# Sums of raw weight blocks on GpSimd instead of VectorE in a hybrid decoder layer

## The chip, the cores and the metric

The kernel runs on one core of a Trainium2 chip. A core has four compute engines with a queue of their own each: TensorE (PE in the profile; its weight loads are PEld), VectorE (DVE), ScalarE (ACT) and GpSimd (POOL). SyncE (SP) issues the loads from memory. Every engine works through its queue in order, and instructions of different engines wait for each other by semaphores. The metric is the device time of one execution in microseconds, as the median of several runs.

## The reference, cut to what matters

One layer of a hybrid decoder on 256 tokens of width 2048: a recurrent branch and an attention branch side by side, merged by gates, then a SwiGLU block and a gated per-layer input. Nearly all of the work is products of activations (256 rows) with large float32 weight matrices:

```
h = rmsnorm(x, g_mix[i])
proj = h @ w_in[i]
x_r, g_r, q, k, v, gate_r, gate_a = jnp.split(proj, IN_SPLIT_POINTS, axis=-1)
...
y_r = y_r @ w_rnn_out[i]
...
x = x + mix @ w_o[i]
h = rmsnorm(x, g_ffn[i])
gu = h @ w_ffn_gu[i]
g, u = jnp.split(gu, 2, axis=-1)
x = x + (jax.nn.silu(g) * u) @ w_ffn_down[i]
ple_gate = jax.nn.sigmoid(rmsnorm(x, g_ple[i]) @ w_ple_gate[i])
x = x + ple_gate * (p[i] @ w_ple_proj[i])
```

## The kernel before, in words

**Weights in two parts.** Every weight block is loaded as float32 by SyncE in chunks of up to 128 x 1024 (tile `w`, four buffers). ScalarE makes a rounded high part of it (`whi`, line 233) and VectorE the low part, weight minus high part (`wlo`, line 234); there are four buffers of each. TensorE then forms each product out of three matmuls, high by high, high by low, low by high (lines 496 to 498 in `prod`). High and low parts of a chunk are made in program order three chunks ahead of TensorE's use (`need`: the 3 is `ahead_split`), and loads run four chunks further ahead (`ahead_dma`). So a chunk's high part can start once TensorE has finished the chunk four places earlier and given its buffers back.

**Groups and slots.** In the token-major stages a group makes 256 tokens x 1024 columns of an output. It is a list of slots, each of which uses one chunk. A slot with a number is a row block of the weights of 128 x 1024: four products (two column halves, two token halves), twelve matmuls. In a group with seven products, four row blocks and their eight quarters are multiplied in the way of Strassen and Winograd: instead of eight products of blocks there are seven, of sums of blocks. These are the slots with letters; each has two products, six matmuls:

```
SEVEN = [0, 1, 2, 3, "11", 8, "21", 9, "22", 10, "T1", 11, "T2", 12, "T3", 13, "T4", 14, 15]
```

`SEVEN_FIRST` has "11", "21" and "22" next to each other, `LONG` has the lettered slots after four numbered ones and more numbered ones behind. The groups with seven products are the two of the recurrent output (`ro`, with `LONG`), two of v, two of the output projection (`wo`), eleven of gate and up (`gu`) and the first of the per-layer gate (`pg`): 18 groups.

**The sums of raw blocks.** The four quarter blocks 11, 21, 22 and 12 (the last is loaded in slot T1) lie in four tiles named X, of a ring of seven. `summed` (line 206) gives the block whose parts a slot needs. For 11, 21 and 22 that is the block as loaded. For T1 to T4 it first adds two tiles in place: T1 is R = 11 + 12, T2 is R = R + 22, T3 is 12 = 12 + 22, T4 is R = R + 21, with R the tile of 11. Line 217 is this addition, over 128 x 1024 float32. Since R is written in place, the sum for T1 must wait until the parts of 11 have been made, the one for T2 until those of T1 have, and the one for T4 until those of T2 have; T3 writes the tile of 12 and must only come behind T1. `split_to` then makes the parts of the result. The order on each engine is laid by the tile framework's scheduler, which may put an instruction ahead of others of its queue when it is ready early.

Other work on these engines in the same stretch: VectorE adds the products' results out of PSUM (line 301, the helper `tt`) and scales them (line 304, `stt`); ScalarE applies Silu, Sigmoid, squares and copies (line 307, `actv`). In the first recurrent output group VectorE also finishes the last recurrent gates (`rnn_gates`, lines 636 to 646).

Of the kernel before, what the change touches and what calls it, by code (L numbers as in the profile page):

```python
# [11 lines left out]
ALU = mybir.AluOpType  # L12
# [162 lines left out]
class Stream:  # L175
# [30 lines left out]
    def summed(self, mode):  # L206


        r = self.raw
        if mode[0] != "T":  # L210
            if mode == "11":
                r["R"] = r["11"]
            return r[mode]
        if mode == "T1":
            r["12"] = r["T1"]
        o, a = {"T1": ("R", "12"), "T2": ("R", "22"), "T3": ("12", "22"), "T4": ("R", "21")}[mode]
        self.nc.vector.tensor_tensor(r[o], r[o], r[a], ALU.add)  # L217
        return r[o]

    def split_to(self, n):  # L220
# [884 lines left out]
```

## Time and profile before

| | |
|---|---|
| median of 3 runs | 1898.63 us (1896.6 to 1898.97) |
| span of the profiled execution | 1897.5 us |
| TensorE busy | 1885.3 us |
| VectorE busy | 1356.5 us |
| ScalarE busy | 1114.1 us |
| GpSimd busy | 2.2 us, 9 instructions |
| sums of line 217 | 72, 88.0 us on VectorE |

The profile is of one execution. A timeline row gives start and duration in us, engine, line of the kernel, operation, what is written and read, how many instructions the row holds, and in brackets the idle time before it and what ended that. A row of groups ends with busy time, mean ns of one, and idle time before. A row of waits reads: engine and what waited, for whom, total us, times, longest. A row of windows gives a stretch, its length, the busy us of PE, PEld, DVE, ACT and POOL with their instructions, the granted clock of TensorE as a share of full speed, the DMA engines' busy share and GB/s.

### The profile page before, as it was taken

Reading aid. Unit: us, or ns where it says so; the run is one execution under the profiler, and the core shown is the slowest. Engines: PE = TensorE matmul, PEld = TensorE weight load, DVE = VectorE, ACT = ScalarE, POOL = GpSimd, SP = SyncE. Lnnn points to the kernel's source line nnn. Section 1 sums busy time; section 2 is a strip of 40 time slices with the busy share of each in tenths; the row PEclk is TensorE's granted clock in tenths of the full one; section 3 lists DMA queues with packets and bytes.
Section 4 is the critical chain, followed back from the end, with each engine's and each line's share of the span. In section 5 each row is a group of like instructions: output and inputs, shape, how many; then the busy total and the mean of one; then the engine's idle time right before and its main releaser. Section 6 shows DMA issues by size and latency. Waiting matters only on the chain.

```text
span 1897.5 us, 24029 instructions
## 1 busy us (share of the span) xinstructions
PE 1885.3 (99%) x9045; PEld 1585.9 (84%) x9045; DVE 1356.5 (71%) x1618; ACT 1114.1 (59%) x1447; POOL 2.2 (0%) x9
## 2 busy tenths in 40 slices
PE   8999999999999999999999999999999999999998
PEld 7988888888888888888888888888888888888887
DVE  7867686877787576665568888865786577865784
ACT  6878686874455576676345755543554355544663
POOL 0000000000000000000000000000000000000000
PEclk9999999999999999999999999999999999999999
DMA  6555555656554554545575555565556555555654
GB/s 238 183 200 182 197 178 194 209 186 217 212 185 168 189 165 156 166 158 175 195 269 183 184 199 191 199 219 178 188 189 223 188 188 189 177 178 191 220 161 149
DMA packets 101781, 361.37 MB, mean 190 GB/s; under 512 B 11424, under 2 KB 11808, under 8 KB 101664
## 3 DMA queue, kind: packets, MB, share of 16 engines
q1 hardware_dynamic: 101520, 359.82, 56.0%
q8 instruction: 71, 1.16, 0.2%
q14 instruction: 46, 0.38, 0.1%
q10 hardware_dynamic: 144, 0.01, 0.0%
HBM read 357.69 MB, written 2.10 MB: 190 GB/s over the span
## 4 chain that ended last, share of the span: by engine, by line
PE 97%; DVE 1%; DMA 1%; ACT 1%; issue 0%; SPq 0%; DVEq 0%; ACTq 0%
PE ps L497 26%; PE ps L498 26%; PE ps L496 26%; PE ps L426 8%; PE ps L430 4%; PE ps L409 1%; PE ps L410 1%; PE ps L408 1%; DMA w<-in_w_dram 1%; PE ps L995 1%; PE ps L786 0%; PE ps L935 0%; DVE wlo L234 0%; DVE T L301 0%; ACT L307 0%
## 5 line engine op out<-in xcount | busy, mean ns | idle before, releaser
L234 DVE TENSOR_TENSOR wlo<-w,whi 128x1024 fp32r<-128x1024 f32 (+3 forms) x606 | 731.7, 1215 | 383.8 <-ACT whi L233 382.0
L233 ACT ACTIVATE whi<-w 128x1024 fp32r<-128x1024 f32 (+3 forms) x606 | 635.9, 1053 | 585.5 <-PE ps L498 515.1
L497 PE MATMUL ps<-wlo,B 128*128 128x512 f32 x1130 | 441.5, 391 | 0.7 <-DVE wlo L234 0.7
L498 PE MATMUL ps<-whi,B 128*128 128x512 f32 x1130 | 441.0, 390 | 0.0
L496 PE MATMUL ps<-whi,B 128*128 128x512 f32 x1130 | 390.5, 393 | 0.1
L497 PE MATMUL ps<-wlo,A 128*128 128x512 f32 x946 | 369.6, 391 | 0.0
L498 PE MATMUL ps<-whi,A 128*128 128x512 f32 x946 | 368.6, 390 | 0.0
L496 PE MATMUL ps<-whi,A 128*128 128x512 f32 x946 | 353.0, 392 | 0.0
L496 PEld LDWEIGHTS ps<-whi,B 128*128 128x128 f32 x1130 | 212.3, 188 | 43.9 <-ACT whi L233 0.6
L498 PEld LDWEIGHTS ps<-whi,B 128*128 128x128 f32 x1130 | 212.3, 188 | 43.9
L497 PEld LDWEIGHTS ps<-wlo,B 128*128 128x128 f32 x1130 | 212.5, 188 | 43.6 <-DVE wlo L234 1.1
L498 PEld LDWEIGHTS ps<-whi,A 128*128 128x128 f32 x946 | 177.8, 188 | 36.6
L497 PEld LDWEIGHTS ps<-wlo,A 128*128 128x128 f32 x946 | 177.9, 188 | 36.1 <-DVE wlo L234 0.4
L496 PEld LDWEIGHTS ps<-whi,A 128*128 128x128 f32 x946 | 177.8, 188 | 35.9
L233 ACT ACTIVATE whi<-X 128x1024 fp32r<-128x1024 f32 x126 | 133.7, 1061 | 70.0 <-PE ps L498 57.8
L426 PE MATMUL ps<-A,whi 128*128 128x512 f32 x704 | 172.1, 394 | 1.6 <-ACT whi L233 1.6
L234 DVE TENSOR_TENSOR wlo<-X,whi 128x1024 fp32r<-128x1024 f32 x126 | 154.2, 1224 | 24.5 <-ACT whi L233 21.7
L426 PEld LDWEIGHTS ps<-A,whi 128*128 128x128 f32 x704 | 129.9, 190 | 26.8 <-ACT whi L233 2.1
L301 DVE TENSOR_TENSOR T<-ps,T 128x512 f32<-128x512 f32 (+1 forms) x160 | 91.1, 611 | 27.6 <-ACT T L307 16.7
L430 PEld LDWEIGHTS ps<-A,wlo 128*128 128x128 f32 x704 | 90.6, 191 | 7.3 <-DVE wlo L234 3.7
L430 PE MATMUL ps<-A,wlo 128*128 128x256 f32 x704 | 92.3, 284 | 3.1 <-DVE wlo L234 2.7
L217 DVE TENSOR_TENSOR X<-X,X 128x1024 f32<-128x1024 f32 x72 | 88.0, 1222 | 1.4
(158 smaller groups left out, 1421.4 us busy)
## 6 DMA issues: line engine op xcount, KB each, us to landing
w<-in_w_dram SPq DMA_DIRECT2D x584, 512.0 KB, 3.8
X<-in_w_dram SPq DMA_DIRECT2D x72, 512.0 KB, 4.6
w<-in_w_dram SPq DMA_DIRECT2D x16, 448.0 KB, 3.3
C<-in_x_dram SPq DMA_DIRECT2D x8, 256.0 KB, 4.2
out_dram<-T SPq DMA_DIRECT2D x8, 256.0 KB, 3.3
C<-in_xT_dram SPq DMA_DIRECT2D x7, 256.0 KB, 7.9
w<-in_w_dram SPq DMA_DIRECT2D x4, 320.0 KB, 3.6
w<-in_w_dram SPq DMA_DIRECT2D x2, 256.0 KB, 3.2
```

Source lines behind the costliest of these rows:

```text
L217: self.nc.vector.tensor_tensor(r[o], r[o], r[a], ALU.add)
L233: self.hi_ins = self.nc.scalar.activation(hi[:, :c], t[:, :c], AF.Copy)
L234: self.lo_ins = self.nc.vector.tensor_tensor(lo[:, :c], t[:, :c], hi[:, :c].bitcast(F32), ALU.subtract)
L301: nc.vector.tensor_tensor(o, a, b, op)
L408: nc.tensor.matmul(o, wt[0], xh, start=start, stop=False)
L409: nc.tensor.matmul(o, wt[0], xl, start=False, stop=False)
L410: nc.tensor.matmul(o, wt[1], xh, start=False, stop=stop)
L426: nc.tensor.matmul(pss[e], wt[0], rhs(xs, k), start=(k == 0), stop=(k == n - 1))
L430: nc.tensor.matmul(pss[e][:, :256], wt[1], rhs(xs, k)[:, :256], start=False, stop=False)
L496: nc.tensor.matmul(ps, x[0], wh, start=start, stop=False)
L497: nc.tensor.matmul(ps, x[0], wl, start=False, stop=False)
L498: nc.tensor.matmul(ps, x[1], wh, start=False, stop=stop)
```

## The change

The addition of line 217 is issued on GpSimd's queue instead of VectorE's. Operands, shapes, order of the calls and everything else stay.

```
         o, a = {"T1": ("R", "12"), "T2": ("R", "22"), "T3": ("12", "22"), "T4": ("R", "21")}[mode]
-        self.nc.vector.tensor_tensor(r[o], r[o], r[a], ALU.add)
+        self.nc.gpsimd.tensor_tensor(r[o], r[o], r[a], ALU.add)
         return r[o]
```

## The prediction

> **What bounds the kernel now.** I read the busy table of the page first, then the chain of waits, then who waited for whom.
>
> ```profile
> span 1897.5 us, 24029 instructions
> ...
> PE 1885.3 (99%) x9045; PEld 1585.9 (84%) x9045; DVE 1356.5 (71%) x1618; ACT 1114.1 (59%) x1447; POOL 2.2 (0%) x9
> ...
> PE 97%; DVE 1%; DMA 1%; ACT 1%; issue 0%; SPq 0%; DVEq 0%; ACTq 0%
> ...
> L217 DVE TENSOR_TENSOR X<-X,X 128x1024 f32<-128x1024 f32 x72 | 88.0, 1222 | 1.4
> ```
>
> TensorE is busy for 99% of the span and makes 97% of the chain. So the 88.0 us that leave VectorE (72 sums, L217) are not in the time today, except where TensorE waits for VectorE. The list of waits shows how little that is:
>
> ```profile
> ACT whi L233 <- PE ps L498: 572.9, 424, 2.8
> ACT whi L233 <- DVE X L217: 3.7, 3, 1.9
> PE ps L497 <- DVE wlo L234: 0.7, 1, 0.7
> ```
>
> TensorE waited once for a low part in a token-major stage, 0.7 us. ScalarE waited 424 times for TensorE to give a buffer back: the splits run as far ahead as four buffers allow. ScalarE waited for a sum three times, 3.7 us. The change can therefore win next to nothing; the question is whether the slower path eats the lead of the splits.
>
> **The lead in a usual group.** The timeline of VectorE and ScalarE in the fourth group of the gate and up stage, around T2 and T4:
>
> ```profile
> 1225.03 1.23 DVE L234 TENSOR_TENSOR wlo<-X,whi 128x1024 fp32r<-128x1024 f32 x1
> 1226.29 1.23 DVE L217 TENSOR_TENSOR X<-X,X 128x1024 f32<-128x1024 f32 x1
> 1227.75 1.23 DVE L234 TENSOR_TENSOR wlo<-w,whi 128x1024 fp32r<-128x1024 f32 x1 [0.24 <-ACT whi L233]
> 1229.15 1.23 DVE L234 TENSOR_TENSOR wlo<-X,whi 128x1024 fp32r<-128x1024 f32 x1 [0.18 <-ACT whi L233]
> 1230.42 1.22 DVE L217 TENSOR_TENSOR X<-X,X 128x1024 f32<-128x1024 f32 x1
> 1232.10 1.22 DVE L234 TENSOR_TENSOR wlo<-w,whi 128x1024 fp32r<-128x1024 f32 x1 [0.46 <-ACT whi L233]
> ...
> 1226.65 1.06 ACT L233 ACTIVATE whi<-w 128x1024 fp32r<-128x1024 f32 x1 [1.66 <-PE ps L498]
> 1228.06 1.06 ACT L233 ACTIVATE whi<-X 128x1024 fp32r<-128x1024 f32 x1 [0.34 <-PE ps L498]
> ```
>
> Low part of T1, sum for T2 (R += 22) at 1226.29, low part of slot 11, low part of T2, sum for T4, low part of slot 12. ScalarE's high parts wait for TensorE, that is, for the buffer of four slots earlier. Between that and the use of the new parts lie three slots. TensorE starts a product's three matmuls every 0.68 us:
>
> ```profile
> 1880.05 0.39 PE L496 MATMUL ps<-whi,B 128*128 128x512 f32 x1
> ...
> 1880.73 0.39 PE L496 MATMUL ps<-whi,B 128*128 128x512 f32 x1
> ```
>
> A numbered slot has four products, 2.72 us, a lettered one two, 1.36 us. A numbered slot between lettered ones is thus split 1.36 + 2.72 + 1.36 = 5.44 us ahead and needs 1228.98 - 1226.65 = 2.33 us: a margin of 3.1 us. A lettered one has 6.8 us ahead, a margin of 4.5 us.
>
> **Part one: 72 sums leave VectorE.** In the usual group they lie under TensorE's work (margin above), so removing them is worth nothing there; VectorE was not late. In the first group of the recurrent output it is late:
>
> ```profile
> 406.07 1.23 DVE L234 TENSOR_TENSOR wlo<-X,whi 128x1024 fp32r<-128x1024 f32 x1 [2.48 <-ACT whi L233]
> 407.21 0.42 DVE L636 TENSOR_SCALAR T<-T 128x512 f32<-128x512 f32 x1
> 407.55 1.22 DVE L217 TENSOR_TENSOR X<-X,X 128x1024 f32<-128x1024 f32 x1
> 408.68 1.22 DVE L234 TENSOR_TENSOR wlo<-w,whi 128x1024 fp32r<-128x1024 f32 x1
> 409.82 1.22 DVE L217 TENSOR_TENSOR X<-X,X 128x1024 f32<-128x1024 f32 x1
> 410.95 0.69 DVE L304 SCALAR_TENSOR_TENSOR T<-T,T 128x512 f32<-128x512 f32 x1
> 411.55 1.22 DVE L234 TENSOR_TENSOR wlo<-X,whi 128x1024 fp32r<-128x1024 f32 x1
> ...
> 410.47 0.39 PE L497 MATMUL ps<-wlo,B 128*128 128x512 f32 x1
> ...
> 415.85 0.51 PE L497 MATMUL ps<-wlo,B 128*128 128x512 f32 x1 [0.66 <-DVE wlo L234]
> ```
>
> Here the low part of slot 4 (408.68 to 409.90) is read at 410.47: a margin of 0.57 us. A little later TensorE stands still for 0.66 us. Two sums, T1 and T3, stand in this queue, 1.14 us from start to start each. If they went away at no cost, TensorE would win that 0.66 us.
>
> **Part two: 72 sums on GpSimd.** No sum of this form has run there. Its nearest rows:
>
> ```profile
> L352 POOL MEMSET w1l<- 128x512 f32 x1 | 0.6, 607 | 0.0
> L352 POOL MEMSET w1h<- 128x512 f32 x1 | 0.5, 524 | 0.3 <-POOLq L1093 0.3
> L363 POOL TENSOR_SCALAR_AFFINE_SELECT negt<-T 128x256 f32<-128x256 f32 x1 | 0.4, 401 | 0.0
> L357 POOL TENSOR_SCALAR_AFFINE_SELECT T<-ones 128x128 f32<-128x128 f32 x1 | 0.3, 288 | 0.0
> ```
>
> Below: VectorE's 1.22 us. The two selects give (401 - 288) / 128 = 0.88 ns per column, so 1024 columns of one input take 1.08 us, of two inputs read one after the other some 2.0 us. Above: the slower memset, 607 / 512 = 1.19 ns per column, once for each of two reads and a write: 3.6 us. I take 2.44 us, twice VectorE's row and the middle of 1.2 and 3.6. The Trainium skill (GPSIMD Engine Reference, Elementwise — side-by-side cycle accounting) gives 4497 ns for an add of 2048 columns; half of it is an estimate of 2.25 us, by which the sum below would be 0.4 us less.
>
> **Part three: do the two engines hinder each other?** GpSimd's sum and VectorE's low part each read two SBUF tiles. The trace has no such pair. Bounds: no hindrance, or each stops the other for its whole length. The only hint is in the first microseconds:
>
> ```profile
> 0.80 0.52 POOL L352 MEMSET w1h<- 128x512 f32 x1 [0.29 <-POOLq L1093]
> 1.26 0.61 POOL L352 MEMSET w1l<- 128x512 f32 x1
> ...
> 1.10 0.30 DVE L348 CAST ones_r<-ones 128x128 fp32r<-128x128 f32 x1
> 1.32 0.27 DVE L360 MEMSET T<- 128x256 f32 x1
> ```
>
> The second memset, with more of VectorE's work beside it, took 0.09 us longer than the first. I take the exclusive end, since it is these reads that would meet. The Trainium skill (SBUF — State Buffer, Who interferes with whom) speaks against this change in the same sense: a VectorE instruction with two SBUF inputs and a GpSimd instruction that reads SBUF share one read interface, whoever starts first keeps it for the whole instruction, and the other is blocked. No row of this trace shows it; by that rule the time is the one below, without it that of the first rival.
>
> Usual group, exclusive: the sum for T2 holds VectorE from 1226.29 to 1228.73, so slot 11's low part is 1.0 us late and T2's high part, due at 1228.06, 0.7 us. T2's low part ends about 1231.1, the sum for T4 runs to 1233.5, slot 12's low part is 1.4 us late. All below 3.1 us: no stall, price nothing. In letters with D for the sum, the last delay is 2D - 3.5; it passes 3.1 at D = 3.3.
>
> First group of the recurrent output, exclusive: the low part of 11 ends at 407.30; T1's sum runs to 409.74, T3's to 412.18, and slot 4's low part starts then instead of at 408.68, 3.5 us late against a margin of 0.57: TensorE stalls 2.9 us. The next low part keeps the 0.69 us instruction in front of it but has lost a sum (1.14 us), so what follows is 3.5 - 1.14 = 2.4 us late, and the 0.66 us stall of before is taken up in it. Net: 2.4 us.
>
> Such a stall has a second price. Early in the run TensorE stood still for 1.87 us, and the granted clock of the stretch after it was halved:
>
> ```profile
> 28.03 1.22 PE L430 MATMUL ps<-A,wlo 128*128 128x256 f32 x8 [1.87 <-DVE wlo L234]
> ...
> 29.60:33.00 3.40, 3.40 (x10) 2.63 (x9) 2.39 (x3) 0.67 (x1) 0.00 (x0) 0.50 0.88 266
> ```
>
> 3.4 us at half the clock cost 1.7 us of work. A 2.9 us stall is longer, so I add 1.7 us; the bounds are 0 and 1.7.
>
> The three places where ScalarE waits for a sum today get at most 1.2 us more each, 3.7 us if all of it reached TensorE; the slots behind have two to three microseconds of lead, so I take 0 and keep 3.7 for the range.
>
> **Queues and DMAs.** GpSimd's queue is empty after the first 3 us, so nothing stands behind the sums there but sums. On ScalarE, behind a high part that waits for a sum, stand the next slot's high part and the Silu, square and copy instructions of the group before; they are late by the 0.7 us above. The change issues no DMA. SyncE's load into the tiles of 21 and 22 now waits for GpSimd's read to end, some 2 us later, with seven chunks of lead. New semaphore waits between GpSimd and ScalarE lie in that lead too.
>
> **Sum.** 2.4 + 1.7 + 0 = 4.1 us on the profiled span of 1897.5 us gives 1901.6; the median of the runs is 1.1 us above that span, so 1902.7 us.
>
> **Rivals.**
> First, not slower: the two engines read side by side. Then slot 4's low part moves ahead of 408.68 and the 0.66 us stall goes: 1898.0 us. For it: the memsets and VectorE's first instructions did run at the same time. Against it: the length of the second memset, and that none of those four reads two tiles. It decides as soon as VectorE's low parts beside a sum keep their 1.22 us. More than this can't be won: TensorE waits for nothing else here.
>
> Second, the sum is long, D near 3.6 and exclusive. One group lasts 43.15 us:
>
> ```profile
> 1205.00:1248.15 43.15, 43.15 (x196) 35.69 (x195) 34.74 (x36) 23.04 (x24) 0.00 (x0) 1.00 0.58 197
> ```
>
> VectorE is busy 34.7 us of it; without four sums of 1.14 us it is 30.2, and with four holds 30.2 + 4 x 3.6 = 44.6, over 43.15 by 1.4. Seventeen groups cost 25 us, the first one 2 x 3.6 - 1.38 - 1.14 = 4.7, the clock 1.7: 1930 us. It decides at D = 3.2. For it: the memset's rate. Against it: the selects' rate.
>
> Third, the order: before, T3's sum ran in front of T2's. If GpSimd's queue has it behind, two holds follow each other from 1226.29 to 1231.17; slot 11's low part is 3.4 us late, 0.3 over its margin, and with T4's hold after that slot 12's 3.8, 0.7 over. Seventeen times 0.7 is 12 us: with 4.1, 1915 us. Against it: T3 was ready early and its engine is now free.
>
> **How the numbers follow.** About 0.2%, 3.8 us, is what a measurement of this kernel can tell from no change. Forecast 0.50: 1900 to 1907, of it 0.30 slower by more than that (with the halved clock, or a sum above 2.4 us) and 0.20 within (without them). Side by side 0.22: 0.16 within, 0.06 faster. Long sum 0.20: slower. Order 0.08: 0.05 slower, 0.03 within, if only some groups have it. Together faster 0.06, within 0.39, slower 0.55. The range goes from 1896.8, below the side-by-side case, to 1920, which leaves out the upper part of the long sums, about 0.1, and what the side-by-side case may win beyond.
>
> **What would show it.** L217 on GpSimd with a mean of 2.2 to 2.7 us, and single low parts (L234) on VectorE stretched to 2 to 3.5 us where one runs: exclusive. All at 1.22 us: side by side. A TensorE wait of 2 to 3 us for a low part near 410 us and a granted clock of 0.5 right behind it: the sum above. Waits for low parts in every gate and up group would show the long sum or the order; starts of the sums tell these two apart. The prediction is wrong in kind if TensorE's waits do not grow at all, or if they grow outside the groups with seven products.

## The result and the profile after

The changed kernel takes 1906.68 us (median of 4 runs, 1905.95 to 1907.14) against 1898.08 us before on the same chip: 8.6 us more, a ratio of 1.0047 with an interval of 1.0035 to 1.0060. Its profiled execution has a span of 1904.9 us, 7.4 us over the one of before.

From the page of the changed kernel, the busy table and the groups that answer to those of before:

```profile
span 1904.9 us, 24079 instructions
...
PE 1888.7 (99%) x9045; PEld 1584.5 (83%) x9045; DVE 1374.0 (72%) x1546; ACT 1112.3 (58%) x1447; POOL 197.6 (10%) x81
...
L234 DVE TENSOR_TENSOR wlo<-w,whi 128x1024 fp32r<-128x1024 f32 (+3 forms) x606 | 798.4, 1325 | 392.7 <-ACT whi L233 390.2
...
L217 POOL TENSOR_TENSOR X<-X,X 128x1024 f32<-128x1024 f32 x72 | 195.4, 2714 | 1627.9 <-DVE wlo L234 1470.3
```

The 72 sums have left VectorE, and yet VectorE is busy for longer, 1374.0 us instead of 1356.5. It gave up 88.0 us and got 105.5 us back: its other instructions are stretched. The low parts of loaded tiles went from 731.7 to 798.4 us; with those of the X tiles (154.2 to 184.8) that is 97 of the 105.5. What such a stretched instruction waits for is not shown as a wait; it is inside its own duration.

From the list of what TensorE waited for, the rows of the token-major stages:

```profile
PE ps L497 <- DVE wlo L234: 5.7, 7, 1.6
...
PE ps L496 <- ACT whi L233: 0.8, 2, 0.5
```

There are seven waits for low parts instead of one, 5.7 us instead of 0.7, and two for high parts, 0.8 us, where there was none. Three stretches hold nearly all of the loss. Both traces have 9045 matmuls, so the start of the n-th matmul can be compared; the difference is set to zero at 400 us, because the start of the run is not the same from one execution to the next (here it was 1.0 us shorter after the change than before, which is why 8.4 us of loss make 7.4 us of span). The loss by starts is larger than the recorded waits: a matmul is recorded with 0.39 us while the next one starts after 0.23 us, so each recorded wait lacks some 0.16 us.

```
stretch                                     loss, us
first recurrent output group (ro 0)         3.47
second output projection group (wo 1)       2.09
first gate and up group (gu 0)              2.51
first per-layer gate group (pg 0)           0.31
the other 14 groups and the rest after 400   0.00
```

**The first recurrent output group.** The timeline of the changed kernel, VectorE, then GpSimd, then TensorE where it waits:

```profile
405.05 1.23 DVE L234 TENSOR_TENSOR wlo<-X,whi 128x1024 fp32r<-128x1024 f32 x1 [2.48 <-ACT whi L233]
406.19 0.42 DVE L636 TENSOR_SCALAR T<-T 128x512 f32<-128x512 f32 x1
406.80 3.16 DVE L234 TENSOR_TENSOR wlo<-w,whi 128x1024 fp32r<-128x1024 f32 x1 [0.18 <-ACT whi L233]
409.88 2.88 DVE L304 SCALAR_TENSOR_TENSOR T<-T,T 128x512 f32<-128x512 f32 x1
412.80 0.69 DVE L301 TENSOR_TENSOR T<-T,T 128x512 f32<-128x512 f32 x1
413.41 1.22 DVE L234 TENSOR_TENSOR wlo<-X,whi 128x1024 fp32r<-128x1024 f32 x1
...
406.36 5.85 POOL L217 TENSOR_TENSOR X<-X,X 128x1024 f32<-128x1024 f32 x2 [403.56 <-DVE wlo L234]
...
410.01 0.50 PE L497 MATMUL ps<-wlo,B 128*128 128x512 f32 x1 [0.62 <-DVE wlo L234]
414.68 0.50 PE L497 MATMUL ps<-wlo,B 128*128 128x512 f32 x1 [1.61 <-DVE wlo L234]
417.73 0.50 PE L497 MATMUL ps<-wlo,B 128*128 128x512 f32 x1 [0.71 <-DVE wlo L234]
420.89 0.50 PE L497 MATMUL ps<-wlo,X 128*128 128x512 f32 x1 [0.76 <-DVE wlo L234]
```

T1's sum starts at 406.36. The low part of slot 4 is issued at 406.80 and ends at 409.96, 3.16 us instead of 1.22: it stood until the sum was over at about 408.8, then ran. T3's sum came next and caught the instruction behind, a 128x512 one of 0.69 us that now takes 2.88. The two sums and the low part between them make 5.85 us: 2.4 + 1.0 + 2.4. TensorE waits four times, 3.70 us together, where it waited once for 0.66 us before.

**A usual group.** The same slots as shown of before, in the fourth gate and up group (low parts of T1, 11, T2, 12; sums for T2 and T4):

```profile
1232.13 1.22 DVE L234 TENSOR_TENSOR wlo<-X,whi 128x1024 fp32r<-128x1024 f32 x1 [0.18 <-ACT whi L233]
1234.80 2.12 DVE L234 TENSOR_TENSOR wlo<-w,whi 128x1024 fp32r<-128x1024 f32 x1 [1.45 <-ACT whi L233]
1236.96 1.23 DVE L234 TENSOR_TENSOR wlo<-X,whi 128x1024 fp32r<-128x1024 f32 x1
1239.11 2.65 DVE L234 TENSOR_TENSOR wlo<-w,whi 128x1024 fp32r<-128x1024 f32 x1 [0.92 <-ACT whi L233]
...
1233.43 2.40 POOL L217 TENSOR_TENSOR X<-X,X 128x1024 f32<-128x1024 f32 x1 [8.31 <-DVE wlo L234]
1238.27 2.40 POOL L217 TENSOR_TENSOR X<-X,X 128x1024 f32<-128x1024 f32 x1 [2.43 <-DVE wlo L234]
```

Here the sum takes 2.40 us, and the low parts beside it are 0.9 and 1.4 us longer than 1.22. TensorE does not notice: the loss of this group is 0.00. The same holds for T1's and T3's sums ahead of them, which stretch two low parts to 2.61 and 3.21 us.

**The second output projection group.** Two high parts of ScalarE before the change, the second one that of T2:

```profile
1043.58 1.06 ACT L233 ACTIVATE whi<-w 128x1024 fp32r<-128x1024 f32 x1 [1.71 <-PE ps L498]
...
1054.65 1.05 ACT L233 ACTIVATE whi<-X 128x1024 fp32r<-128x1024 f32 x1
```

After the change, where the group starts 2.45 us later than before, ScalarE, then GpSimd and VectorE:

```profile
1043.86 0.46 ACT L307 ACTIVATE B<-ps,prm_sb 128x256 fp32r<-128x256 f32 x1
1047.99 0.47 ACT L307 ACTIVATE B<-ps,prm_sb 128x256 fp32r<-128x256 f32 x1 [3.68 <-DVE B L304]
1048.37 1.05 ACT L233 ACTIVATE whi<-w 128x1024 fp32r<-128x1024 f32 x1
...
1062.43 0.63 ACT L307 ACTIVATE X<-T 128x512 fp32r<-128x512 f32 x1 [4.74 <-POOL X L217]
...
1040.77 5.71 POOL L217 TENSOR_TENSOR X<-X,X 128x1024 f32<-128x1024 f32 x2 [22.16 <-DVE wlo L234]
1057.69 4.71 POOL L217 TENSOR_TENSOR X<-X,X 128x1024 f32<-128x1024 f32 x1 [11.21 <-DVE wlo L234]
...
1044.16 3.40 DVE L234 TENSOR_TENSOR wlo<-X,whi 128x1024 fp32r<-128x1024 f32 x1
1047.49 0.47 DVE L304 SCALAR_TENSOR_TENSOR B<-ps,prm_sb,B 128x256 fp32r<-128x256 f32 x1
...
1057.73 0.68 DVE L301 TENSOR_TENSOR B<-T,B 128x512 fp32r<-128x512 f32 x1
1058.33 0.68 DVE L301 TENSOR_TENSOR C<-C,T 128x512 f32<-128x512 f32 x1
1058.93 1.22 DVE L234 TENSOR_TENSOR wlo<-w,whi 128x1024 fp32r<-128x1024 f32 x1
```

This group also normalizes the next stage's activations, in pairs of a ScalarE and a VectorE instruction that wait for each other. T3's sum stretches a low part to 3.40 us, the VectorE half of a pair comes at 1047.49, and ScalarE stands for 3.68 us before it reaches the next high part, at 1048.37, 2.3 us late. Ten microseconds on, T2's sum is itself the one that waits: VectorE has three instructions back to back that read two SBUF tiles each, the last one ends at 1060.15, and the end of the sum (1057.69 + 4.71 = 1062.40) lies 2.25 us behind that, nearly the length of a sum. ScalarE's next instruction writes an X tile and is released by this sum; it stands for 4.74 us with T2's high part behind it, which starts at 1062.97, 5.9 us late.

**The first gate and up group** has the same pairs and, ahead of them, the scales of the normalization, one per token. The row of their last small addition, from the changed kernel's groups by form (before: 156 ns each; the other one of the two stands in the first per-layer gate group):

```profile
L301 DVE TENSOR_TENSOR ssq<-ssq 128x2 f32<-128x2 f32 x2 | 4.8, 2389 | 0.1
```

Two columns take 2.39 us, the length of a sum. ScalarE's logarithm, table loads and high parts stand behind it. On the lead that is left, T2's and T4's sums then stretch the low parts of slots 9 and 10, and TensorE waits 0.73 and 0.89 us for these two:

```profile
1099.94 0.87 DVE L304 SCALAR_TENSOR_TENSOR B<-ps,prm_sb,B 128x256 fp32r<-128x256 f32 x2
1100.74 2.84 DVE L234 TENSOR_TENSOR wlo<-w,whi 128x1024 fp32r<-128x1024 f32 x1
...
1105.86 3.21 DVE L234 TENSOR_TENSOR wlo<-w,whi 128x1024 fp32r<-128x1024 f32 x1
...
1100.10 2.40 POOL L217 TENSOR_TENSOR X<-X,X 128x1024 f32<-128x1024 f32 x1 [5.80 <-DVE wlo L234]
1105.58 2.40 POOL L217 TENSOR_TENSOR X<-X,X 128x1024 f32<-128x1024 f32 x1 [3.08 <-DVE wlo L234]
```

The first row shows what is not held: its second instruction lies wholly inside T2's sum, reads PSUM and one SBUF tile, and keeps its 0.48 us.

Two things come together in this group and in the first per-layer gate group: the scales, and an order of slots (`SEVEN_FIRST`) that only these two have. They were not told apart. The second output projection group has the usual order.

### The profile page after: what moved, and what is told of

It reads as the page before. It is cut to its first block, busy times and chain, and to the rows that moved or that the text cites. A ratio compares the mean times of both kernels' runs of the same rounds, so it can differ in the third digit from the quotient of the medians.

```text
span 1904.9 us, 24079 instructions
## 1 busy us (share of the span) xinstructions
PE 1888.7 (99%) x9045; PEld 1584.5 (83%) x9045; DVE 1374.0 (72%) x1546; ACT 1112.3 (58%) x1447; POOL 197.6 (10%) x81
## 5 line engine op out<-in xcount | busy, mean ns | idle before, releaser
L234 DVE TENSOR_TENSOR wlo<-w,whi 128x1024 fp32r<-128x1024 f32 (+3 forms) x606 | 798.4, 1325 | 392.7 <-ACT whi L233 390.2
L217 POOL TENSOR_TENSOR X<-X,X 128x1024 f32<-128x1024 f32 x72 | 195.4, 2714 | 1627.9 <-DVE wlo L234 1470.3
L234 DVE TENSOR_TENSOR wlo<-X,whi 128x1024 fp32r<-128x1024 f32 x126 | 184.8, 1466 | 23.4 <-ACT whi L233 21.6
```

Source lines behind the costliest of these rows:

```text
L217: self.nc.gpsimd.tensor_tensor(r[o], r[o], r[a], ALU.add)
L234: self.lo_ins = self.nc.vector.tensor_tensor(lo[:, :c], t[:, :c], hi[:, :c].bitcast(F32), ALU.subtract)
```

## The experiments

The loss by stretch of every run, worked out as above, and the median against that of the runs of before on the same chip:

```
run                                      ro 0   wo 1   gu 0   rest   sum    median, difference
changed kernel                           3.47   2.09   2.51   0.31   8.38   +8.6
T1, T3 on GpSimd                         3.47   0.00   0.38   0.01   3.86   +3.5
T2, T4 on GpSimd                         0.00   0.00   0.00   0.00   0.00   -0.2
15 groups on GpSimd                      0.02   0.00   0.00   0.29   0.31   +0.4
3 groups on GpSimd                       3.43   2.07   3.23   0.00   8.73   +8.8
halves of 512 columns                    3.30   0.00   2.10   0.41   5.81   +5.7
T1, T3, T4 on GpSimd                     3.42   0.00   0.91   0.00   4.33   +4.0
extra reads, sums on VectorE             1.95   2.33   3.90   3.69  11.87  +10.7
four sums back                           0.01   0.00   0.76   0.35   1.12   +1.2
before, T1 and T3 late in ro 0           0.73   0.00   0.00   0.00   0.73   +1.0
```

### Only the early sums, only the late sums

T1 and T3 are made early in the queue, T2 and T4 right before they are needed.

```
+        eng = self.nc.gpsimd if mode in ("T1", "T3") else self.nc.vector
+        eng.tensor_tensor(r[o], r[o], r[a], ALU.add)
```

> Only the sums for T1 and T3 on GpSimd, those for T2 and T4 on VectorE. Theory of the held read path (a sum on GpSimd stops a VectorE instruction that reads two SBUF tiles, for up to 2.4 us, and costs time where that instruction had no lead): the first recurrent output group loses 3 to 4 us as with all four, since its loss came from the low part of slot 4 behind T1 and T3; the second output projection group loses nothing; the first gate and up group part of its 2.5 us. In all 4 to 6 us over before. Rival, the length of the sum alone (ScalarE waits 2.4 instead of 1.2 us for a block, above all for T2 and T4): 0 to 1 us over before. Single low parts are stretched to about 3 us under the first, all stay at 1.2 us under the rival.

Measured: 1900.74 us against 1897.22 (ratio 1.0020, interval 1.0011 to 1.0029), 3.47 us in the first recurrent output group as with all four, 0.38 in the first gate and up group. Low parts go up to 3.4 us. The total is a little below the range expected, and the first gate and up group lost less than expected.

The second run has `("T2", "T4")` in that line.

> Only the sums for T2 and T4 on GpSimd, those for T1 and T3 on VectorE. Theory of the held read path: first recurrent output group 0 to 1 us, second output projection group about 2 us, first gate and up group 1 to 2.5 us: 2 to 5 us over before. Rival, the length of the sum alone: nearly all of the 8.6 us, since only these two sums have ScalarE waiting for them.

Measured: 1897.03 us, no difference (0.9991 to 1.0009), and no loss in any group, though T2's and T4's sums are those for which ScalarE waits:

```profile
L218 POOL TENSOR_TENSOR X<-X,X x36: 2397/2403/5055, 419.4 to 1812.3; 128x1024 f32<-128x1024 f32 x36
...
  ACT whi L234: 21.4, 17
```

These are the sums' line in this run (shortest, median, longest in ns) and who waited for them: ScalarE, 17 times, 21.4 us, as in the changed kernel (21.6 us in 18). The rival falls: a sum that is twice as long costs nothing by its length, as long as T1's and T3's are on VectorE. The expectation of the first theory falls too: neither half has a loss in the second output projection group, and 0.38 us is all that they have in the first gate and up group, where all four make 2.5. The loss of these two groups needs both.

### Where it is lost

```
+        three = at in (("ro", 0), ("wo", 1), ("gu", 0))
+        eng = self.nc.gpsimd if not three else self.nc.vector
+        eng.tensor_tensor(r[o], r[o], r[a], ALU.add)
```

> GpSimd's sums in 15 groups; in the first recurrent output group, the second output projection group and the first gate and up group they are on VectorE. Theory (60 sums lie in the lead of the splits): 0 to 0.6 us over before, less than a measurement tells, though low parts in these groups are stretched. Rival, the cost is spread over the kernel (a changed order on the engines, or a toll on every sum): 15/18 of 8.6, about 7 us.

Measured: 1897.61 us against 1897.22 (0.9992 to 1.0009). Sixty sums on GpSimd cost 0.31 us in the trace, though low parts are stretched to 3.4 us there too.

The counterpart has `if three`.

> GpSimd's sums only in the first recurrent output group, the second output projection group and the first gate and up group, 12 of 72. Theory: 7.5 to 9 us over before, all of the loss. Rival, a spread cost: 3/18 of 8.6, about 1.4 us.

Measured: 1906.05 us (1.0032 to 1.0058), 8.8 us over before. Twelve sums make the whole loss (the first gate and up group loses 3.23 us here, 0.7 more than in the changed kernel; why is open); a toll on every sum or a cost spread by a changed order is excluded.

### Is it the path to SBUF?

Two kernels leave the sums on VectorE and add work on GpSimd whose result nobody uses.

```
         self.nc.vector.tensor_tensor(r[o], r[o], r[a], ALU.add)
+        self.nc.vector.tensor_copy(self.col, self.dum[:, :1])
+        for _ in range(2):
+            self.nc.gpsimd.tensor_tensor(self.dum, self.src, self.src, ALU.add)
```

> All sums stay on VectorE. Behind each one GpSimd adds a scratch tile of 480 columns to itself, twice, two inputs from SBUF, some 2.2 us, and nobody waits for the result; a one-column copy on VectorE starts it. Theory of the held read path: VectorE's two-input instructions beside it are stretched (low parts up to 3 us) and the time rises by 2 to 12 us, since VectorE still has its 88 us of sums. Rival, the cost comes from waiting for the sum and not from the shared path: no low part is stretched, 0 to 1 us over before (72 copies of one column are under 5 us of VectorE, under its lead).

> As the run before, but GpSimd writes the scratch tile four times (memset, some 2.2 us in all) and reads nothing. If it is the read path that is held: no low part is stretched, 0 to 1 us over before. If any access of GpSimd to SBUF holds VectorE up: stretched low parts and the same time as the run before.

The second one has four `memset(self.dum, 0.0)` in place of the two additions. Both missed their place: nothing ties the copy to the sum, so the scheduler put this work into the recurrent stage, the last of it at 340 us. There the two still differ as expected. VectorE's products with `rstd`, two SBUF inputs, from the groups by form of the run that reads and of the run that writes:

```profile
L304 DVE TENSOR_TENSOR T<-T,rstd 128x256 f32<-128x256 f32 x44 | 29.6, 708 | 0.0
```

```profile
L304 DVE TENSOR_TENSOR T<-T,rstd 128x256 f32<-128x256 f32 x44 | 16.9, 418 | 0.0
```

They took 418 ns in the run that writes, as in the kernel before, and 708 ns in the run that reads. Of the low parts of 128x1024, 61 ran beside a write for over 0.1 us and none took over 1.23 us; 53 ran beside an addition in this way, and 23 of these took over 1.3 us, up to 2.01. The times, 1948.62 us (+50.5) and 1900.61 us (+2.5), lie above the ranges expected and are no clean measure, since VectorE's one-column copy also waits for GpSimd to be done with the scratch tile, 39.9 us in the first and 26.8 us in the second; the durations are. What is held is the reading side, as far as a memset and an addition differ in nothing else that matters here; a GpSimd instruction that reads one tile was not tried.

The third kernel of this kind reads the blocks themselves, so that it must come behind each sum:

```
+        for _ in range(2):
+            self.nc.gpsimd.tensor_tensor(self.dum, r[o][:, :480], r[a][:, :480], ALU.add)
```

> The sums stay on VectorE; behind each one GpSimd reads 480 columns of its two blocks into a scratch tile, twice, so that it runs in the same stretches as the moved sums did, and ScalarE, VectorE and TensorE wait for none of it except to write the block again. Theory of the held read path: low parts beside it are stretched, and the loss stands in the same groups: 3 to 5 us in the first recurrent output group, 3 to 12 us in all. Rival, the loss comes from waiting for the sum on GpSimd: 0 to 1 us over before.

Measured: 1908.05 us against 1897.31 (1.0036 to 1.0070), the loss in the same three groups and 3.7 us in the others; low parts up to 2.3 us. The sums are on VectorE here, so nothing of this comes from a sum on GpSimd; but GpSimd's reads stretch them too, to 1.36 us in the mean and 2.25 at most. The first recurrent output group lost 1.95 us, less than expected. Part of the total is VectorE's own wait to write a block that GpSimd still reads, 21.8 us in the list, so the 10.7 us are an upper bound for the reads alone.

### Shorter holds

```
+        for s in (slice(0, 512), slice(512, 1024)):
+            self.nc.gpsimd.tensor_tensor(r[o][:, s], r[o][:, s], r[a][:, s], ALU.add)
```

> All 72 sums on GpSimd, each as two instructions of 512 columns. Theory of the held read path with the waiting engine next in turn: a hold lasts 1.2 us, a VectorE instruction runs between two holds, no low part takes over 2.5 us; the first recurrent output group loses 1 to 3 instead of 3.5 us, in all 2 to 6 us over before. Rival, the total length of the sum counts: 8.6 us or more, for the two instructions together are no shorter than one.

Measured: 1903.81 us against 1898.10 (1.0021 to 1.0040). A half takes 1.30 us, no low part over 2.32 us, and the loss is 5.8 instead of 8.4 us. The gain is in the second output projection group above all; the first recurrent output group keeps 3.30 us, more than was expected: with two halves per sum there are four holds in front of the same few VectorE instructions, 7.01 us from the first to the last instead of 5.85.

### T2 back on VectorE

```
+        eng = self.nc.vector if mode == "T2" else self.nc.gpsimd
+        eng.tensor_tensor(r[o], r[o], r[a], ALU.add)
```

> T1, T3 and T4 on GpSimd, T2 on VectorE. In the changed kernel's second output projection group T2's sum took 4.7 us and ScalarE stood before it. Theory: that group's 2.1 us and most of the 2.3 us at T2 and T4 of the first gate and up group need T2's sum on GpSimd on top of what T1 and T3 had already delayed; without it 3.5 us in the first recurrent output group and 0 to 1 us elsewhere, 3.5 to 4.5 us over before. Rival, T4 or the changed order does it: 6 to 8.6 us.

Measured: 1902.12 us against 1898.10 (1.0012 to 1.0031): 3.42 us in the first recurrent output group, nothing in the second output projection group, 0.91 in the first gate and up group. With the early and the late sums this shows what the loss of these two groups is made of. How late the latest low part of a group ends, against the kernel before shifted by the loss up to that group, in us:

```
run                      ro 0   wo 1   gu 0   fourth gate and up group
changed kernel            4.6    5.5    6.3   2.0
T1, T3 on GpSimd          4.3    2.9    3.6   2.0
T2, T4 on GpSimd          2.0    1.7    3.3   1.3
T1, T3, T4 on GpSimd      4.3    3.3    4.3   2.0
```

Up to 3.3 us late there is no loss, and from 3.6 us on there is one, near the margin of 3.1 us that was worked out for a usual group. The early sums use up most of the lead, and T2's sum, late behind VectorE's stream and with ScalarE standing before it, then has too little. Whether it is the sum's wait for VectorE or ScalarE's wait for the X tile that weighs more was not tried.

### Four sums back

```
+        back = {("ro", 0): ("T1", "T3"), ("wo", 1): ("T2",), ("gu", 0): ("T2",)}.get(at, ())
+        eng = self.nc.vector if mode in back else self.nc.gpsimd
```

> The changed kernel with four sums back on VectorE: T1 and T3 of the first recurrent output group, T2 of the second output projection group and of the first gate and up group; the other 68 on GpSimd. Theory: the 8.4 us are made at these places, so 0.5 to 1.5 us over before is left. Rival, the loss moves to the next places: 4 us or more.

Measured: 1898.53 us against 1897.31 (0.9999 to 1.0017), 1.12 us in the trace. Moving four of 72 sums back took away over 7 of the 8.4 us, and the loss did not move on.

### The order in the first recurrent output group

The kernel before has its only token-major waits of TensorE here. All sums on VectorE, T1's and T3's held behind the low part in front of them:

```
+        if at == ("ro", 0) and mode in ("T1", "T3"):
+            with self.tc.issue_after(self.lo_ins.ins):
+                self.nc.vector.tensor_tensor(r[o], r[o], r[a], ALU.add)
```

> Before, all sums on VectorE, but in the first recurrent output group T1's and T3's are kept behind the low part of the slot in front of them instead of early in the queue. If the lead of the low parts is what counts there, TensorE's wait of 0.66 us near 416 us goes and the time falls by 0.5 to 1.3 us, less than a measurement tells, to be read from TensorE's waits. Rival, the wait has another cause: TensorE's waits stay as before.

Measured: 1898.26 us against 1897.31 (0.9995 to 1.0014), 0.73 us more in the trace. TensorE, where it waits:

```profile
414.70 0.50 PE L502 MATMUL ps<-wlo,B 128*128 128x512 f32 x1 [0.24 <-DVE wlo L238]
417.86 0.50 PE L502 MATMUL ps<-wlo,X 128*128 128x512 f32 x1 [0.76 <-DVE wlo L238]
422.54 1.21 PE L501 MATMUL ps<-whi,B 128*128 128x512 f32 x4 [0.30 <-ACT whi L237]
```

The wait moved and grew, which neither expectation had. In the kernel before VectorE is busy for 15.6 of the 18 us from 405 to 423 us; that this is why the order of two sums does not help is likely, and not shown. No kernel here is faster than the one before by more than a measurement tells.

## Why the prediction was right, and where it was not

**Bound and gain: right.** TensorE stays at 99%, and taking 88.0 us from VectorE brought nothing. The sign came from taking the exclusive end for two engines that read side by side.

**The sum's length: right.** 2.44 us were taken, the median is 2.404 us (the mean of 2.71 us includes the time that sums stood behind VectorE). The estimate from the Trainium skill (GPSIMD Engine Reference, Elementwise — side-by-side cycle accounting), 2.25 us, is 6% low.

**Exclusive or side by side: right.** Low parts stretched to 3.4 us, unchanged ones beside writes, a loss with the sums still on VectorE: the three runs with added work show that it is the reads. This agrees with the Trainium skill (SBUF — State Buffer, Who interferes with whom), down to the exception for an instruction that only writes. The first rival falls; so do the third, since T3's sum runs right behind T1's and ahead of T2's, and the second, since the sum is 2.4 us long.

**The usual group at no price: right, also in its terms.** Delays of 1.0 and 1.4 us were worked out for the low parts of slots 11 and 12; 0.9 and 1.4 were measured, below the margin of 3.1. The run with 15 groups confirms it: 0.31 us for 60 sums. T1's and T3's sums were not worked out for this group; they made low parts up to 2.0 us late, also without loss.

**First recurrent output group: the mechanism right, the terms not.** 2.4 us were taken and 3.47 measured. The prediction let T3's sum follow T1's directly; in the trace the waiting VectorE instruction comes between, and T3's sum catches the next one instead, so the loss is spread over four waits. The second term, 1.7 us for a halved clock after one long stall, did not come at all: the longest wait is 1.61 us, and the sign that was named for it, a wait of 2 to 3 us with a clock of 0.5 behind it, is absent. From the windows of the changed kernel (the last three figures are granted clock, DMA share and GB/s):

```profile
408.00:424.00 16.00, 12.30 (x50) 8.75 (x49) 14.39 (x13) 9.84 (x12) 4.66 (x3) 1.00 0.25 71
```

TensorE is busy for 12.3 of 16 us, in pieces, and its clock stays at 1.00. What one wait of 2.9 us would have done to the clock is not shown. The two errors nearly cancel, which is luck: 4.1 predicted, 3.47 measured.

**The step that failed:** "All below 3.1 us: no stall, price nothing", worked out in one usual group and taken for all seventeen, and with it "the slots behind have two to three microseconds of lead, so I take 0 and keep 3.7 for the range". The second output projection group, counted among the usual ones, lost 2.09 us; of the three places where ScalarE waited for a sum before, one is in the first gate and up group, which lost 2.51, and one in the first per-layer gate group, which lost 0.31. With it falls "they are late by the 0.7 us above", said of ScalarE's other work: in the second output projection group ScalarE stood for 3.68 and 4.74 us. The runs show that the sum's length by itself costs nothing (late sums alone: 0.00), and that the margin is used up where VectorE and ScalarE also make the next stage's activations: a stretched VectorE instruction holds up ScalarE there, and ScalarE the high parts. The early sums alone cost 0.38 us in these groups, early and late ones together 4.6: the delays share one lead. This missing term, 4.6 us and 0.31 in the first per-layer gate group, is, to within 0.3 us, what lies between the 4.6 us by which the forecast is above this median of before and the 8.6 measured, less the 0.6 us that the first recurrent output group cost below its forecast. That 1906.68 still falls between 1900 and 1907 is in part luck: the upper part of that stretch was meant for a halved clock or a sum above 2.4 us, and neither came.

## What to carry to other kernels

An engine that is idle is no free place for an addition if it reads memory through the path of the engine it is to relieve: count how long it holds that path (2.4 us here) against what it takes away (1.14 us here), and look for its price in the durations of the other engine's instructions, since no wait is shown. A lead that absorbs one delay is used up by it: work out the margin in the groups that carry extra work, and add up all the delays that fall within one lead.

## What the runs showed of the hardware that was not expected

The two engines can take turns: between two sums one behind the other on GpSimd, the waiting VectorE instruction ran, 5.85 us for 2.4 + 1.0 + 2.4. But a sum can also be kept out: beside VectorE instructions without a gap it waited through three of them, 4.71 us in place of 2.40, and 5.06 us in the run with the late sums.

The size of the held instruction did not matter: an addition of two columns that reads two SBUF tiles went from 156 to 2389 ns. What it reads did: an instruction on PSUM and one SBUF tile, inside a sum, kept its 0.48 us.
